# A hybrid decoder layer: program order for the load queue of the mixer, five weight pieces ahead, deferred stores, rotary tables first, norms and adaLN as small streams

## The chip, the cores and the metric

The kernel runs on one core of a Trainium2 chip. The metric is the device time of one execution in microseconds. TensorE (PE in the profile), VectorE (DVE), ScalarE (ACT), GpSimd (POOL) and SyncE (SP) run side by side; SP issues nearly all DMA transfers, in the order of its instruction queue.

## The reference

One layer, sequence S = 2048, width D = 1024, float32 throughout, cut to what matters:

```python
mod = silu(c) @ w_ada + b_ada                      # 6 vectors of 1024
shift1, scale1, gate1, shift2, scale2, gate2 = split(mod, 6)
h = rmsnorm(x, norm1_w) * (1 + scale1) + shift1
q, k, v, z, xbc, dt_raw = split(h @ w_in)          # 512, 128, 128, 512, 1024, 8 columns
q, k = rope(q, positions), rope(k, positions)
attn = sliding_window_attention(q, k, v, sinks)    # 8 heads, window 128
xbc = silu(causal_depthwise_conv(xbc, conv_w, conv_b))
xs, B, C = split(xbc)
dt = softplus(dt_raw + dt_bias)
y = ssd_chunked_scan(xs, dt, A, B, C, d_skip) * silu(z)
y = group_rmsnorm(y) * ssm_norm_w
x = x + gate1 * (concat(attn, y) @ w_out)
h = rmsnorm(x, norm2_w) * (1 + scale2) + shift2
x = x + gate2 * ((silu(h @ w_gate) * (h @ w_up)) @ w_down)   # inner width 2816
return rmsnorm(x, final_norm_w)
```

## The kernel before

The sequence is cut into four blocks of 512 tokens (`b` = 0 to 3). Activations lie with channels on the partitions: `h` is a list of eight slices of 128 channels, each a pair of tiles (a rounded part and the remainder), and every dense product is three matmuls, high by high, high by low, low by high (`mm3`, lines 237 to 240).

**Mixer phase.** For each block `norm1` makes `h`; then `queries`, `keys_values`, `convolved` and `gated` multiply it with the columns of `w_in`. Their results (q, k/v, convolved channels, z) go to DRAM. `attentions` and `ssds` read them back by tiles of 128 tokens as side streams; their results go to DRAM too (`spill`), and `out_proj` reads them for the output projection, which leaves `mid` (the residual stream) and a running sum of squares for the second norm. All dense products use four PSUM banks (`dense`); each side stream step uses one of four others (`side_bank`). `out_proj` of blocks 2 and 3 and the attention and scan that they need run beside the FFN.

**Weights** come in pieces (`weight`, line 222): at first use a piece is loaded raw, ACT makes the rounded part, POOL the remainder, and the pair is stored to DRAM; later blocks load the pair. There are six buffers for pairs (`SPLIT`) and five for raw pieces (`RAW`). The functions ask for a piece where they use it.

**Order.** Each of the functions is a Python generator. `run(main, ratio)` steps the dense stream; after each step `tick` counts down delayed actions (`pending`), steps the remaining adaLN columns once, and steps the side streams `ratio` times on average. Inside `manual_schedule` blocks the named engines keep the program's order: PE in the mixer, and PE, DVE and SP in the first norm. Everything else is ordered by a planner, which simulates the program with its own costs: SP in the mixer, all engines in the FFN, and DVE, ACT and POOL almost everywhere.

**First norm** (`first_norm`, line 929). x of block 0 is loaded; ACT squares it and PE sums the squares with 64 two-column matmuls (line 942); `root_of` and `spread` make the factor. The adaLN columns for shift1 and scale1 (`ada`, line 151: a load of 512 KB and one long DVE reduction, line 154) are made slice by slice between the modulations (lines 274 to 277). Then `rope_tables` (line 177) makes sine and cosine on DVE, which `rope` (lines 321 to 324) needs.

**The other 32 adaLN columns** (`ada_later`, line 156) are two loads of 256 KB and two reductions each (lines 160 and 165), through two buffers per half.

**FFN.** `operands` makes combinations of the normed blocks, `quads` the up projection (seven products in place of eight, lines 803 to 805), `down` the down projection; lines 709 and 772 load `spill` and `mid`.

Of the kernel before, what the change touches and what calls it, by code (L numbers as in the profile page):

```python
# [17 lines left out]
P = 128  # L18
# [12 lines left out]
TMP, M1, M2, M4 = 9, 3, 8, 4  # L31
# [11 lines left out]
def hymba_layer(ctx, tc, xT, crow, pos, wada, vecs, rows, wq, wkv, wz, wx, wo, wgu, wd4, wd2, outT):  # L43
# [29 lines left out]

    class tiles:
# [14 lines left out]
    common, extra = tiles(sb, M1, M2, M4), tiles(xp, 3, 10, 4)  # L89
# [7 lines left out]
    def const(shape, name, dt=F32, pool=sb):  # L97
        return pool.tile(shape, dt, name=name, tag=name, bufs=1)
# [57 lines left out]
    def ada_later(i):  # L156
# [4 lines left out]
        for _ in range(3):  # L161
            yield
# [14 lines left out]
    def rope_tables():  # L177
# [6 lines left out]
        for dst, turn in ((sin, 0.0), (cos, 0.25)):  # L184
# [8 lines left out]
            nc.scalar.activation(dst.rearrange("p t j -> p (t j)"), r, AF.Sin)  # L193

# [27 lines left out]
    def weight(src, n, key, store):  # L222
# [12 lines left out]
        return hi, lo  # L235

# [35 lines left out]
    def modulated(x, bc, scale, shift, into):  # L272
        h = tmp()
        nc.vector.scalar_tensor_tensor(h, x, scale, bc, ALU.mult, ALU.mult)
        hi, lo = into
        nc.scalar.activation(hi, h, AF.Identity, bias=shift)
        nc.vector.scalar_tensor_tensor(lo, h, shift, hi.bitcast(F32), ALU.add, ALU.subtract)  # L277
        return hi, lo
# [47 lines left out]
    def tokens(b, h, name, srcs, n, toks):  # L326
# [3 lines left out]
        for kp in range(KT // 2):  # L330
            whi, wlo = weight(srcs[kp], 2 * n, (name, kp), b == (0 if name[0] == "z" else 1) and toks[-1] == NT - 1)
# [10 lines left out]
    def queries(b, h):  # L342
        if b == 0:
            qb = [dense() for _ in range(NT)]
            for kp in range(KT // 2):
                ws = first_ws[kp] if kp < len(first_ws) else [weight(wq[c][kp], 512, (f"q{c}", kp), False)
                                                              for c in range(2)]
# [9 lines left out]
            for t, ps in enumerate(qb):  # L357
                q = extra.m2()
                rope(q, ps, 8, t)
                nc.sync.dma_start(q_d[t], q)  # L360
            return
        for part in range(2):
            for t, ps in (yield from tokens(b, h, f"q{part}", wq[part], 256, range(NT))):
                q = staged()
                rope(q, ps, 4, b * NT + t)
                nc.sync.dma_start(q_d[b * NT + t][:, part * 256:part * 256 + 256], q)
            yield

    def keys_values(b, h):
        dt_of[b] = small([P, NT, 8], "dt", 3)  # L370
        for half in range(2):
            for t, ps in (yield from tokens(b, h, "kv", wkv, 264, (2 * half, 2 * half + 1))):
# [4 lines left out]
                nc.sync.dma_start(kv_d[b * NT + t], kv)  # L377
            yield

    def convolved(b, h):  # L380
        for c in range(8):
            ps = dense()
            for half in range(2):
                if half:
                    yield
                whi, wlo = weight(wx[c, half], T, ("x", c, half), b == 0)
# [16 lines left out]
            nc.sync.dma_start(xs_d[b][c], o)  # L403
            yield

    def gated(b, h):
        for part in range(2):
            for t, ps in (yield from tokens(b, h, f"z{part}", wz[part], 256, range(NT))):
# [3 lines left out]
                nc.sync.dma_start(z_d[b * NT + t][:, part * 256:part * 256 + 256], z)  # L412
# [50 lines left out]
    def attentions(b, m):  # L463
        late = []

        def values_of(sms, slots, t):
# [8 lines left out]
            def sums(half):  # L475
# [3 lines left out]
                if half:  # L479
                    nc.sync.dma_start(spill[b][0:4, :, t * P:(t + 1) * P].rearrange("c p t -> p c t"),  # L480
                                      got["out"].rearrange("p (c t) -> p c t", c=4))
            return turn, sums

        held = None
        for t in range(NT):
            gt = b * NT + t
            q, kv = m.m2(), m.m1()
            nc.sync.dma_start(kv, kv_d[gt])
            nc.sync.dma_start(q, q_d[gt])
# [19 lines left out]
            for j in range(4):  # L509
# [3 lines left out]
                if j == 3:  # L513
                    probabilities(st, sms, slots)
                yield
# [74 lines left out]
    def ssds(b, stepping, m):  # L590
        dt, ahi, alo, ex = yield from stepping
        ub = upper.unsqueeze(1).broadcast_to([P, 4, P])
# [21 lines left out]
        def turned(y, o, ts):  # L614
# [6 lines left out]
            nc.sync.dma_start(dst[4:8, :, ts].rearrange("c p t -> p c t"), o3)  # L621

        for t in range(NT):
            ts = slice(t * P, (t + 1) * P)
            xl, z = m.m4().bitcast(F32).rearrange("p h t -> p (h t)").rearrange("p (c t) -> p c t", c=8), m.m2()
            nc.sync.dma_start(xl, xs_d[b][:, :, ts].rearrange("c p t -> p c t"))
            nc.sync.dma_start(z, z_d[b * NT + t])
# [40 lines left out]
            yield  # L668
            st = bank("st", 1)
# [22 lines left out]
            nc.vector.tensor_scalar(ss, ss, 1.0 / 256, EPS, ALU.mult, ALU.add)  # L692
            rs = small([P, 2], "rs", 2)
# [11 lines left out]
    def out_proj(b, y_of, into, bank_of, norm=None):  # L705
        mix = []
        for c in range(KT):
            m = tmp()
            nc.sync.dma_start(m, spill[b][c])
            mix.append(split(m, into(c)))  # L710
            if c % 4 == 3:
                yield
        acc = tmp()
        for c in range(KT):
            ps = bank_of(c)
            for half in range(2):
                if half:
                    yield
                whi, wlo = weight(wo[c, half], T, ("o", c, half), b == 0)
# [4 lines left out]
            x = tmp()  # L724
            nc.sync.dma_start(x, xT[b, c])
            nc.vector.scalar_tensor_tensor(x, ps, gate1[:, c:c + 1], x, ALU.mult, ALU.add)
            nc.sync.dma_start(mid[b][c], x)
            square_into(acc, x, c == 0)
            yield

        def root():
            y_of[b] = rstd(acc, st=norm and norm())
        if norm is None:
# [447 lines left out]
```

## Time and profile before

| | |
|---|---|
| median of 3 runs | 2439.05 us (2437.32 to 2443.29) |
| profiled execution, its own time | 2434.49 us |
| its span in the profile | 2432.8 us |
| mean granted PE clock | 0.965 |
| DMA traffic | 403.82 MB, mean 166 GB/s |

In the profile's groups "d<-w,hl" is a product of activations with a weight piece that gives tokens on the partitions (q, k/v, z), "d<-hl,w" one that gives channels (convolution). "issue to landing" of a transfer is from SP's instruction to its arrival. The idle time before an instruction is put down to what ended it.

### The profile page before, as it was taken

What the parts mean: (1) busy time and instruction counts of PE and PEld (TensorE: products, weight loads), DVE (VectorE), ACT (ScalarE), POOL (GpSimd) and SP (SyncE); (2) the same over time, 40 slices, a digit from 0 to 9 for tenths busy, and PEclk for the clock granted to TensorE, in tenths of its full rate; (3) what the DMA queues carried; (4) which work ended last, traced back from release to release, by engine and by line L of the source; (5) the groups of instructions that cost most, each with busy time, mean ns of one, the idle gap of its engine ahead of it and who ended that gap; (6) DMA issues with size and microseconds to landing.
All of it is one profiled execution on the core that took longest, in us unless ns stands there. A gap on an engine that the chain in (4) does not pass through costs nothing.

```text
span 2432.8 us, 33013 instructions
## 1 busy us (share of the span) xinstructions
PE 2261.8 (93%) x11254; PEld 1891.9 (78%) x11254; DVE 1461.9 (60%) x2519; ACT 967.3 (40%) x2004; POOL 1262.3 (52%) x1249
## 2 busy tenths in 40 slices
PE   6587999999999799999999999899899999999996
PEld 5567989887988588888887877677688888878785
DVE  7876874764445965578675434438855555554544
ACT  2354552655245545433334323224333333333332
POOL 3653743534122864679885234137766666643432
PEclk9798999999999799999999999999899999999998
DMA  7699866868874322233235555764322222263441
GB/s 274 210 331 316 294 228 204 279 218 275 287 241 159 96 78 83 81 111 100 88 95 167 197 177 158 249 206 136 130 87 84 86 79 78 78 228 98 145 157 53
DMA packets 244457, 403.82 MB, mean 166 GB/s; under 512 B 21952, under 2 KB 68032, under 8 KB 244288
## 3 DMA queue, kind: packets, MB, share of 16 engines
q1 hardware_dynamic: 243136, 400.66, 50.0%
q8 instruction: 89, 1.46, 0.2%
q10 hardware_dynamic: 1152, 1.05, 0.1%
q14 instruction: 80, 0.66, 0.1%
HBM read 307.19 MB, written 94.44 MB: 165 GB/s over the span
## 4 chain that ended last, share of the span: by engine, by line
PE 77%; DVE 8%; DMA 5%; issue 4%; POOL 3%; ACT 3%; SPq 1%; POOLq 0%; DVEq 0%; ACTq 0%
PE d L238 11%; PE d L240 11%; PE d L239 11%; PE d L803 8%; PE d L805 8%; PE d L804 8%; PE am L238 1%; PE am L239 1%; PE am L240 1%; POOL w L231 1%; PE at L574 1%; DMA t<-act 1%; DMA t<-in_xT_dram 1%; PE sm L683 1%; PE st L803 1%
## 5 line engine op out<-in xcount | busy, mean ns | idle before, releaser
L752 ACT ACTIVATE w<-raw 128x512 fp32r<-128x512 f32 x308 | 193.5, 630 | 531.7 <-PE d L240 251.0
L803 PE MATMUL d<-b,w 128*128 128x512 f32 x924 | 372.7, 405 | 17.4 <-ACT b L783 9.6
L804 PE MATMUL d<-b,w 128*128 128x512 f32 x924 | 370.8, 401 | 7.2 <-DVE b L779 5.1
L805 PE MATMUL d<-b,w 128*128 128x512 f32 x924 | 368.9, 399 | 0.0
L238 PE MATMUL d<-a,w 128*128 128x512 f32 (+1 forms) x720 | 281.1, 398 | 12.4 <-ACT a L871 11.5
L239 PE MATMUL d<-a,w 128*128 128x512 f32 (+1 forms) x720 | 281.5, 391 | 1.7 <-DVE a L747 1.7
L240 PE MATMUL d<-a,w 128*128 128x512 f32 (+1 forms) x720 | 282.3, 392 | 0.0
L753 POOL TENSOR_TENSOR w<-raw,w 128x512 fp32r<-128x512 f32 x88 | 120.1, 1365 | 304.8 <-ACT w L752 292.0
L753 POOL TENSOR_TENSOR w<-s,w 128x512 fp32r<-128x512 f32 x132 | 188.6, 1429 | 126.1 <-ACT w L752 117.6
L882 DVE SCALAR_TENSOR_TENSOR x<-d,mod,x 128x512 f32<-128x512 f32 (+1 forms) x182 | 130.9, 725 | 197.6 <-PE d L240 197.3
L238 PE MATMUL d<-w,hl 128*128 128x256 f32 (+1 forms) x640 | 194.8, 304 | 43.3 <-DVE s L322 19.9
L803 PEld LDWEIGHTS d<-b,w 128*128 128x128 f32 x924 | 175.9, 191 | 60.6 <-ACT b L783 13.3
L753 DVE TENSOR_TENSOR w<-raw,w 128x512 fp32r<-128x512 f32 x220 | 191.1, 869 | 43.3 <-ACT w L752 40.7
L804 PEld LDWEIGHTS d<-b,w 128*128 128x128 f32 x924 | 176.4, 191 | 46.7 <-DVE b L779 6.8
L805 PEld LDWEIGHTS d<-b,w 128*128 128x128 f32 x924 | 176.5, 191 | 39.9
L240 PE MATMUL d<-w,hl 128*128 128x256 f32 (+1 forms) x640 | 190.8, 298 | 4.6 <-DVE hl L277 4.6
L239 PE MATMUL d<-w,hl 128*128 128x256 f32 (+1 forms) x640 | 189.7, 296 | 0.0
L238 PEld LDWEIGHTS d<-a,w 128*128 128x128 f32 x720 | 137.1, 191 | 47.5 <-ACT a L871 15.5
L238 PEld LDWEIGHTS d<-w,hl 128*128 128x128 f32 x640 | 130.8, 204 | 48.4 <-issue 20.9
L239 PEld LDWEIGHTS d<-a,w 128*128 128x128 f32 x720 | 136.8, 190 | 34.4 <-DVE a L747 2.8
L248 POOL TENSOR_TENSOR t<-t 128x512 f32<-128x512 f32 (+1 forms) x84 | 106.7, 1271 | 108.5 <-ACT t L247 104.8
L240 PEld LDWEIGHTS d<-a,w 128*128 128x128 f32 x720 | 136.2, 189 | 30.3
(311 smaller groups left out, 5427.7 us busy)
## 6 DMA issues: line engine op xcount, KB each, us to landing
raw<-in_wgu_dram SPq DMA_DIRECT2D x176, 256.0 KB, 2.7
raw<-in_wd_dram SPq DMA_DIRECT2D x176, 256.0 KB, 2.7
w<-w_x SPq DMA_DIRECT2D x48, 512.0 KB, 4.9
w<-w_o SPq DMA_DIRECT2D x48, 512.0 KB, 4.6
act<-t SPq DMA_DIRECT2D x88, 256.0 KB, 2.1
t<-act SPq DMA_DIRECT2D x88, 256.0 KB, 4.7
t<-in_xT_dram SPq DMA_DIRECT2D x80, 256.0 KB, 4.3
aw<-in_wada_dram SPq DMA_DIRECT2D x64, 256.0 KB, 3.8
```

The costliest lines, as they stand in the source:

```text
L231: nc.gpsimd.tensor_tensor(lo, raw[:, :n], hi.bitcast(F32), ALU.subtract)
L238: nc.tensor.matmul(out, ahi, bhi, start=first, stop=False)
L239: nc.tensor.matmul(out, ahi, blo, start=False, stop=False)
L240: mm3.last = nc.tensor.matmul(out, alo, bhi, start=False, stop=last)
L248: eng.tensor_tensor(acc, acc, sq, ALU.add)
L574: nc.tensor.transpose(ps[:, (2 * s + r) * P:(2 * s + r + 1) * P], sm[:, r, s, :], ident)
L752: nc.scalar.activation(hi, x, AF.Copy)
L753: eng.tensor_tensor(lo, x, hi.bitcast(F32), ALU.subtract)
L803: nc.tensor.matmul(out, ahi, bhi, start=first and k == 0, stop=False, skip_group_check=True)
L804: nc.tensor.matmul(out, ahi, blo, start=False, stop=False, skip_group_check=True)
L805: mm3.last = nc.tensor.matmul(out, alo, bhi, start=False, stop=k == 3, skip_group_check=True)
L882: nc.vector.scalar_tensor_tensor(x, ps, gate2[:, c:c + 1], x, ALU.mult, ALU.add)
```

## The change

- The first norm makes the sine table before anything else on DVE and the cosine table between the sum of squares and the root. The squares are summed by seven DVE adds and four matmuls. q of block 0 goes to two side banks and two dense banks.
- In the mixer phase SP, too, keeps the program's order. All weight pieces of the phase are listed in `plan`, in the order of use; `take_w` hands out the next one and issues loads until five are ahead.
- Stores in the mixer (`put`) are issued one to three steps after the instruction that makes their data.
- `norm1` becomes a stream: one x load per step, then three steps, the root, four steps, and the eight modulations in two halves, each behind a permission (`free`) and behind its four loads. The factor is copied to SBUF. adaLN columns wait four steps in place of three between loads and reductions; they start after q of block 0, behind the last modulation on DVE.
- Side streams load one tile ahead; `out_proj` gets its inputs from a stream of loads (`loads`) and loads x ahead of its matmuls; the dt steps run inside `ssds`.
- Sums of squares have a tile of their own; there are eight temporaries in place of nine, and nine `m2` tiles of the mixer's extra pool in place of ten.

The diff, cut to its core:

```diff
-TMP, M1, M2, M4 = 9, 3, 8, 4
+TMP, M1, M2, M4 = 8, 3, 8, 4
...
+    def sums():
+        return big("acc", 1, pool=fw)
...
-    common, extra = tiles(sb, M1, M2, M4), tiles(xp, 3, 10, 4)
+    common, extra = tiles(sb, M1, M2, M4), tiles(xp, 3, 9, 4)
...
-        for _ in range(3):
+        for _ in range(4):
             yield
...
-            nc.sync.dma_start(split_d[key], two[:, :, :n].bitcast(F32))
+            put(split_d[key], two[:, :, :n].bitcast(F32), 3)
...
+    pending, mixer_phase = [], [True]
+
+    def put(dst, src, ticks):
+        if mixer_phase[0]:
+            pending.append([ticks, lambda: nc.sync.dma_start(dst, src)])
+        else:
+            nc.sync.dma_start(dst, src)
...
+    planned, ahead = plan(), []
+
+    def fetch(n):
+        for _ in range(n):
+            spec = next(planned, None)
+            if spec is not None:
+                ahead.append(weight(*spec))
+
+    def take_w(n=1):
+        fetch(n - len(ahead))
+        got = [ahead.pop(0) for _ in range(n)]
+        fetch(SPLIT - n - len(ahead))
+        return got
...
-    def norm1(b, h):
-        acc = tmp()
+    def norm1(b, h, free):
+        acc, xs = sums(), []
         for d in range(KT):
-            square_into(acc, load_x(b, d), d == 0)
-        yield
+            xs.append(load_x(b, d))
+            yield
+            if d:
+                square_into(acc, xs[d - 1], d == 1)
+        square_into(acc, xs[-1], False)
+        for _ in range(3):
+            yield
         y = rstd(acc)
-        yield
-        bc = spread(y)
-        for d in range(KT):
-            h.append(modulated(load_x(b, d), bc, scl1[:, d:d + 1], sh1[:, d:d + 1], operand()))
-        yield
+        for _ in range(4):
+            yield
+        bc, ps = const([P, T], "bc", pool=ip, bufs=1), spread(y)
+        nc.scalar.copy(bc, ps)
+        for half in range(2):
+            while free[0] <= half:
+                yield
+            xs = [load_x(b, 4 * half + i) for i in range(4)]
+            yield
+            for i in range(4):
+                d = 4 * half + i
+                h.append(modulated(xs[i], bc, scl1[:, d:d + 1], sh1[:, d:d + 1], operand()))
+                if i % 2:
+                    yield
...
-            qb = [dense() for _ in range(NT)]
+            qb = [side_bank(2), side_bank(3), dense(), dense()]
...
-        held = None
+        def load(t):
+            q, kv = m.m2(), m.m1()
+            nc.sync.dma_start(kv, kv_d[b * NT + t])
+            nc.sync.dma_start(q, q_d[b * NT + t])
+            return q, kv
+
+        held, nxt = None, load(0)
+        yield
+        yield
...
+                if j == 2 and t + 1 < NT:
+                    nxt = load(t + 1)
...
     def first_norm():
-        st, h, x0, ws = side_bank(0), [], [], []
+        accs, h, x0, tables = [tmp(), tmp()], [], [], rope_tables()
+        next(tables)
+        for i in range(2):
+            silu_c(i)
...
-        for d in range(2):
-            ada(8 + d, common.m4)
-            ada(d, extra.m4)
         for d in range(KT):
-            sq = tmp()
-            nc.scalar.activation(sq, x0[d], AF.Square)
-            for t in range(NT):
-                nc.tensor.matmul(st[:, 2 * t:2 * t + 2], sq[:, t * P:(t + 1) * P], ones[:, 0:2],
-                                 start=d == 0 and t == 0, stop=d == KT - 1 and t == NT - 1, skip_group_check=True)
+            square_into(accs[d % 2], x0[d], d < 2, nc.vector)
+        acc = accs[0]
+        nc.vector.tensor_tensor(acc, acc, accs[1], ALU.add)
+        st = side_bank(0)
+        for t in range(NT):
+            nc.tensor.matmul(st[:, 2 * t:2 * t + 2], acc[:, t * P:(t + 1) * P], ones[:, 0:2], start=True, stop=True)
+        next(tables)
+        ada(8, common.m4)
+        ada(0, extra.m4)
+        fetch(2)
         y = root_of(st, NT)
...
-        if ada_rest:
-            next(ada_rest[0], None)
+        for g in list(background):
+            if next(g, g) is g:
+                background.remove(g)
...
-    with tc.manual_schedule(engines={mybir.EngineType.PE}):
-        run(queries(0, h), 0)
-        with tc.issue_after(last_load.ins):
-            nxt = norm_ahead(1, (17, 21))
-        rest = rest_of_ada()
-        ada_rest.append(rest)
-        run(keys_values(0, h), 0)
-        prepared(0)
+    with tc.manual_schedule(engines={mybir.EngineType.PE, mybir.EngineType.SP}):
+        with tc.issue_after(first_done.ins):
+            run(queries(0, h), 0)
+            nxt, free = norm_ahead(1, 1)
+            background.append(rest_of_ada())
+            run(keys_values(0, h), 0)
...
+        while background or pending:
+            tick(0)
+        finish(att)
+        while pending:
+            tick(0)
+    mixer_phase[0] = False
```

More of the change, by code (lines that the diff above doesn't have):

```diff
@@ L371, in keys_values @@
         for half in range(2):
-            for t, ps in (yield from tokens(b, h, "kv", wkv, 264, (2 * half, 2 * half + 1))):
+            for t, ps in (yield from tokens(h, 264, (2 * half, 2 * half + 1))):
                 kv = staged()
@@ L385, in convolved @@
                     yield
[L386 removed]
+                (whi, wlo), = take_w()
                 for i in range(4):
@@ L407, in gated @@
         for part in range(2):
-            for t, ps in (yield from tokens(b, h, f"z{part}", wz[part], 256, range(NT))):
+            for t, ps in (yield from tokens(h, 256, range(NT))):
                 z, th = staged(), big("s", 3, pool=fw)[:, 0:256]
@@ L718, in out_proj @@
                     yield
-                whi, wlo = weight(wo[c, half], T, ("o", c, half), b == 0)
+                whi, wlo = weights(c, half)
                 for i in range(4):
```

235 lines of the change are left out of this document (136 added, 99 removed).

## The prediction

> **What bounds the kernel now.** I read the profile's page first, then the busy times of the engines by stage, then who waits for whom inside the stages.
>
> ```profile
> span 2432.8 us, 33013 instructions
> PE 2261.8 (93%) x11254; PEld 1891.9 (78%) x11254; DVE 1461.9 (60%) x2519; ACT 967.3 (40%) x2004; POOL 1262.3 (52%) x1249
> PE   6587999999999799999999999899899999999996
> PEclk9798999999999799999999999999899999999998
> ```
>
> TensorE (PE) is busy for 2261.8 of 2432.8 us, so 171 us of idle time is all that reordering can win directly, and the slices put most of it in the first four (61 us each). The next view cuts the span at the stages: norm of block 0; its q projection; a hole; k/v, convolution and z gate of block 0; q and k/v of block 1; two long stretches of blocks 1 to 3; the change-over to the FFN; three stretches of FFN. Columns: stretch, length, busy us (instructions) of PE, PEld, DVE, ACT and POOL, granted PE clock, DMA share, GB/s.
>
> ```profile
> 0.00:31.00 31.00, 15.86 (x66) 14.23 (x66) 17.11 (x37) 8.60 (x14) 7.54 (x51) 1.00 0.89 340
> 31.00:79.00 48.00, 35.27 (x192) 32.17 (x192) 42.25 (x71) 13.07 (x22) 17.31 (x11) 0.82 0.61 196
> 79.00:98.00 19.00, 0.00 (x0) 0.00 (x0) 18.30 (x30) 6.31 (x10) 10.36 (x8) 0.60 0.61 201
> 98.00:216.00 118.00, 95.42 (x555) 84.77 (x556) 83.34 (x208) 57.88 (x132) 73.67 (x76) 0.91 0.92 316
> 216.00:281.00 65.00, 55.87 (x397) 53.84 (x396) 50.21 (x133) 26.68 (x62) 42.48 (x45) 0.87 0.83 275
> 281.00:603.00 322.00, 307.69 (x1925) 273.81 (x1925) 202.92 (x476) 171.59 (x435) 143.09 (x248) 0.98 0.75 249
> 603.00:782.00 179.00, 177.51 (x1118) 158.39 (x1119) 83.55 (x247) 72.76 (x175) 32.64 (x57) 1.00 0.70 231
> 782.00:832.00 50.00, 32.91 (x129) 22.73 (x128) 47.80 (x59) 33.04 (x74) 38.76 (x26) 0.73 0.32 99
> 832.00:1297.00 465.00, 464.76 (x2283) 387.46 (x2282) 306.71 (x447) 206.65 (x466) 340.37 (x329) 1.00 0.29 92
> 1297.00:1740.00 443.00, 413.42 (x1721) 327.81 (x1719) 241.02 (x334) 144.24 (x238) 191.29 (x136) 0.96 0.54 176
> 1740.00:2433.00 693.00, 663.06 (x2880) 536.64 (x2880) 368.67 (x483) 226.44 (x382) 364.80 (x268) 0.98 0.34 112
> ```
>
> Idle PE by stage: 15.1, 12.7, 19.0, 22.6, 9.1, 14.3, 1.5, 17.1, 0.2, 29.6 and 29.9 us. Block 0 up to the first work of block 1 (216 us) holds 69 of the 171, and it is where DMA is nearest its end (316 GB/s, share 0.92). Who ended PE's waits from 98.5 to 282 us (total, times, longest):
>
> ```profile
> PE d L238 <- DVE s L322: 19.9, 2, 19.6
> PE d L238 <- DVE so L411: 8.6, 2, 6.7
> PE am L493 <- DMA m<-kv: 8.4, 1, 8.4
> PE at L574 <- DVE m L578: 5.4, 1, 5.4
> PE d L238 <- ACT hl L276: 3.6, 2, 2.4
> PE d L240 <- DVE hl L277: 2.6, 3, 1.6
> ```
>
> and three of those from 281 to 782 us, the largest and the only two that a DMA ended:
>
> ```profile
> PE st L617 <- ACT m L697: 4.8, 1, 4.8
> PE at L501 <- DMA m<-q: 0.9, 1, 0.9
> PE d L238 <- DMA w<-w_o: 0.3, 1, 0.3
> ```
>
> Block 0 waits for tables, loads and late evictions; blocks 1 to 3 hardly wait for a transfer (1.2 us in 501). A better order of loads can win early and has next to nothing to win later, where it can only lose.
>
> **The change, part by part.** *Rotary tables first.* The 19.6 us hole ends at the rope of q (L322): k/v cannot start because all four dense banks hold q, and DVE makes the tables only then, with adaLN reductions between. Quiet steps of the tables cost
>
> ```profile
> L191 DVE SCALAR_TENSOR_TENSOR s<-s 128x512 f32<-128x512 f32 x2 | 1.4, 684 | 0.0
> L187 DVE TENSOR_SCALAR s<-s 128x512 f32<-128x512 f32 x1 | 0.4, 427 | 0.0
> ```
>
> so sine or cosine is 4 x 0.43 + 3 x 0.68 = 3.8 us. Sine goes where DVE waits for x; cosine goes between the sum of squares and the root, on the path (3.8 us, counted next). Moreover q of block 0 now takes two side banks, so two dense banks are free and k/v starts at once: -19.6 us. If the cover failed, the rope alone (16 DVE operations on half of L187's elements, so at most 16 x 0.43 = 7 us) would delay the second half of k/v, which needs the two banks behind it.
>
> *First norm.*
>
> ```profile
> 8.33 4.98 ACT L940 ACTIVATE t<-m 128x512 f32<-128x512 f32 x8
> 9.09 13.79 PE L942 MATMUL am<-ones,t 128*128 128x2 f32 x64 [9.09 <-ACT t L940]
> ```
>
> Sixty-four small matmuls end at 22.9 us; in their place are seven adds of DVE (0.68 each, 4.8 us, beside the squares that end at 13.3) and four matmuls, about 16 us. Then cosine (3.8) and two adaLN reductions come before the root: about 22 us, 1 earlier. The loop over the eight slices of h follows, bound by DVE:
>
> ```profile
> L154 DVE CUSTOM_DVE_ANT_0 m<-m,csil,vec 128x1024 f32<-128x1024 f32 x12 | 20.1, 1707 | 0.0
> L277 DVE SCALAR_TENSOR_TENSOR hl<-t,mod,hl 128x512 fp32r<-128x512 f32 x8 | 7.6, 955 | 4.1 <-ACT hl L276 3.7
> L274 DVE SCALAR_TENSOR_TENSOR t<-m,scl,at 128x512 f32<-128x512 f32 x8 | 5.9, 744 | 0.1
> ```
>
> These three are 33.6 of DVE's 42.25 us there; the rest is mostly the later adaLN columns, which now queue behind the last slice. Two L154 more move in behind the root (+3.4), and the wait for ACT that those columns partly filled opens again (3.7 us in the row, up to twice that). Net -1 us, between -5 and +3; with the root -2.
>
> *adaLN and the first x loads as streams.* One 256 KB load pair per five steps of the mixer, where before
>
> ```profile
> L160 SPq DMA_DIRECT2D aw<-in_wada_dram x22: 327/328/382, 16.5 to 96.9; - x22
> L160 SPq DMA_DIRECT2D aw<-in_wada_dram x27: 327/656/2020, 102.6 to 213.6; - x27
> L165 DVE CUSTOM_DVE_ANT_0 aw<-aw,csil,vec 128x512 f32<-128x512 f32 x14 | 15.2, 1085 | 4.9 <-DMA aw<-in_wada_dram 4.9
> L165 DVE CUSTOM_DVE_ANT_0 aw<-aw,csil,part 128x512 f32<-128x512 f32 x13 | 11.4, 876 | 6.9 <-DMA aw<-in_wada_dram 6.9
> ```
>
> (first two: issues up to 98 us and from 98 to 216; then DVE in 98 to 216). Of 49 loads ahead of block 1 about 11 stay: block 0 has 28 steps after q. From 98 to 216 DVE loses some 16 us of work and the 11.8 us that it stood in order before a reduction; DVE's late evictions (8.6, 5.4) hang on that. Bytes: 0.316 x 118 = 37.3 MB moved in that stretch; less 27 x 0.262, plus 11 x 0.262, plus about 3.5 MB (k/v and convolution weights, x) that went during the q stage and the hole: 36.6 MB. How fast can they go? The fastest 20 us:
>
> ```profile
> 140.00:160.00 20.00, 18.61 (x86) 15.01 (x85) 13.01 (x32) 14.87 (x37) 13.66 (x16) 1.00 1.04 381
> ```
>
> At 381 GB/s it is 96 us, at the stretch's own 316 it is 116; PE's own busy time is 95.4. I take 105, the middle, for both limits would have to be met exactly for 96: -13 us. The Trainium skill, "DMA: Bandwidth & Descriptors", section Specifications, puts HBM at about 358 GB/s for a core; by that 36.6 MB take an estimated 102 us and the gain here could not pass 16. The trace's 381 over 20 us is above it, so the measurement sets the floor.
>
> *Norm of block 1* is ready by steps, four slices before the z gate ends: the 3.6 + 2.6 us of waits on hl go, -5. The norm's factor is now copied out of its bank, one ACT operation per block (4.98 / 8 = 0.6 us, with ACT busy 57.88 of 118). Late next is the side attention's DVE work (L574 behind L578), whose loads now come two steps early; POOL keeps all its work (73.67 of 118).
>
> *Queue in program order, five pieces ahead, stores deferred.* SP now holds every load of the mixer behind whatever store or load waits ahead of it: weights, x, q/k/v of the side streams. What covers it:
>
> ```profile
> 166.15 0.40 PE L238 MATMUL d<-hl,w 128*128 128x512 f32 x1
> 166.39 0.39 PE L239 MATMUL d<-hl,w 128*128 128x512 f32 x1
> w<-w_x SPq DMA_DIRECT2D x45, 512.0 KB, 4.8
> SPq L226 <- PE d L240: 99.7, 55, 4.2
> ```
>
> A piece is 12 matmuls at a pitch of 0.23, 2.8 us, so five are 13.8 us; a load lands 4.8 us after issue, which leaves 9 us for holds. SP's most common wait (for PE to free a weight buffer; its rows are those of 281 to 782 us) was 1.8 us on average, 4.2 at most. So the queue is covered, and its cost lies between 0 and, if the 38 displaced adaLN loads (10 MB, 26 us at 381 GB/s) found no room, 26 us; DMA's free quarter of 501 us makes me take 5. The k/v pieces are half as long, hence not 0.
>
> *Rest.* One temporary buffer less, running sums and the norm's broadcast in tiles of their own, the dt steps of blocks 2 and 3 moved into the FFN (some 20 tiny DVE operations beside 465 us in which PE idles 0.2): 0, within -8 to +8. The change-over at 782 is untouched: 0, from -17 (its whole idle time) to +5.
>
> **The sum** is -19.6 - 2 - 13 - 5 + 5 = -35 us. The profiled execution took 2434.49 us, 4.6 below the median of the runs shown, 2439.05 (2437.32 to 2443.29): 2399.5 against the one, 2404 against the other, which I predict.
>
> **Rivals.** *Fuller gain.* If adaLN was what kept block 0 from PE's pace, 118 becomes 95 (-23), the waits on hl go whole (-6), and, DVE being ahead, the change-over closes as well (-17): with -22 from the start, -68, 2371. For it: DVE at 47.80 of 50 us there. Against it: DMA at 0.92 before, and that change-over's work is untouched. Chance 0.14.
>
> *Bytes decide.* The stretch stays at 316 GB/s and 116 us (-2), the displaced loads cost 14 of their 26: -22 - 2 + 14 = -10, 2429. For it the 0.92; against it that much of the waiting was for DVE. Chance 0.10, half of it too small to tell.
>
> *The queue becomes the bound, slower.* From 281 to 782 us there are 128 steps of 3.9 us. Once SP's holds and issues take longer than a step, the lead of five is used up and PE waits at each piece; before, other loads passed the one that waited. If each step then loses 0.6 us, 77 us go against the 40 won: +37, 2476. Decisive is a hold over 9 us, or a mean of over 3.9 per step; the rows show 1.8 for the common one. A rule of the skill is its ground: "DMA: Bandwidth & Descriptors", section on the anatomy of one DMA, says that the DMA engines do not wait on semaphores, so every wait stands in the issuing sequencer. Chance 0.16.
>
> **Numbers.** The forecast itself has 0.60 (2380 to 2419). About 0.3%, 7 us, is what a measurement can tell. Faster: 0.60 + 0.14 + 0.05 = 0.79; the same 0.05; slower 0.16. The range 2360 to 2450 leaves out the end of the fuller gain and most of the slower rival.
>
> **What would show it.** Right: no PE hole before k/v, k/v near 77 us and block 1 near 182; some 11 adaLN loads by then; from there stage lengths within 3% of those above. Wrong: PE waits in blocks 1 to 3 that end at a weight load, SP holds of over 9 us, or a k/v stage that waits for its banks.

## The result and the profile after

The changed kernel takes 2465.65 us (median of 4 runs, 2460.41 to 2470.41) against 2438.19 us of the kernel before beside it (2432.82 to 2443.29): a ratio of 1.0112, 95% interval 1.0082 to 1.0143. It is slower by 27.5 us where 35 us less were forecast. The profiled execution spans 2465.6 us, 32.8 more than the one before.

The top of its profile page, with the same lines as were shown of before:

```profile
span 2465.6 us, 32901 instructions
PE 2263.2 (92%) x11198; PEld 1886.1 (76%) x11198; DVE 1430.0 (58%) x2526; ACT 970.5 (39%) x2009; POOL 1271.5 (52%) x1249
PE   3788999897899699999999999998899999999896
PEclk9899999998999799999999999998899999999998
```

PE has the same work (2263.2 us against 2261.8), so what was lost is idle time: 202 us in place of 171. The slices (61.6 us each) say where: the first is emptier than before, the second and fourth are fuller, the eighth, tenth and eleventh show 8, 7 and 8 where 9s stood, and the fourteenth, the change-over, a 6 for a 7. Busy time by stage (same columns as before), cut at the first and last dense matmuls of this kernel's stages:

```profile
0.00:39.00 39.00, 3.91 (x10) 2.28 (x10) 28.30 (x52) 15.09 (x22) 11.57 (x53) 1.00 0.64 238
83.50:104.00 20.50, 13.46 (x98) 12.95 (x98) 6.87 (x27) 6.11 (x11) 13.33 (x18) 0.83 0.59 205
257.80:580.00 322.20, 301.69 (x1862) 267.55 (x1861) 208.25 (x488) 159.77 (x397) 142.11 (x230) 0.97 0.77 257
580.00:621.00 41.00, 23.62 (x132) 19.23 (x131) 20.14 (x46) 20.63 (x57) 9.81 (x17) 0.73 0.49 170
621.00:666.70 45.70, 39.73 (x300) 38.51 (x300) 19.23 (x79) 6.56 (x14) 11.05 (x25) 0.94 0.81 273
```

and the k/v stage of block 3 in the kernel before:

```profile
633.00:646.00 13.00, 13.00 (x108) 12.85 (x107) 10.00 (x40) 3.88 (x9) 5.07 (x12) 1.00 1.02 385
```

The row to look at is 580 to 621. It holds 132 matmuls in 41 us, nearly all of them the side streams' own, and PE is idle for 17 us of it at a granted clock of 0.73. Before, this stretch, from the output projection of block 0 to q of block 3, lasted 5.5 us. In the next row k/v of block 3 takes 19.8 us of the 45.7, from its first matmul to its last; before it took 13.1 with PE busy throughout. The row from 83.5 is k/v of block 0, 20.5 us of which PE idles 7.

Set against before stage by stage (by the starts of dense products in the two traces; a stage ends where its last three matmuls start), the 32.8 us and the forecast's terms are:

| stretch | forecast | measured |
|---|---|---|
| start to k/v of block 0 (98.3, now 83.6) | -21.6 | -14.7 |
| k/v of block 0 to q of block 1 (117.9 us, now 114.3) | -13 | -3.6 |
| q of block 1 to the end of the output projection of block 0 (381.5, now 382.1) | 0 (-5 and +5) | +0.6 |
| that end to q of block 3 (5.5, now 41.0) | 0 | +35.5 |
| q of block 3 to the end of its z gate (178.1, now 179.7) | 0 | +1.6 |
| change-over and FFN (1651.5, now 1664.9) | 0 | +13.4 |
| sum | -34.6 | +32.8 |

Up to the fourth row the change is 17.7 us ahead. Three causes stand in the trace. The first is the start. ACT's rows, then DVE's, then POOL's (start, duration, what it was idle for):

```profile
12.01 1.28 ACT L197 ACT_TABLE_LOAD   x1
14.99 1.28 ACT L148 ACT_TABLE_LOAD   x1
18.49 1.28 ACT L197 ACT_TABLE_LOAD   x1
```

```profile
16.94 0.69 DVE L149 SCALAR_TENSOR_TENSOR csil<-s,csil 128x512 f32<-128x512 f32 x1 [4.23 <-ACT s L148]
17.55 5.87 DVE L310 TENSOR_TENSOR t<-t 128x512 f32<-128x512 f32 x6
```

```profile
18.03 3.03 POOL L239 TENSOR_TENSOR w<-raw,w 128x512 fp32r<-128x512 f32 x2 [12.34 <-ACT w L238]
```

The sine (L197) now stands between the two halves of silu(c) (L148), so ACT changes its function table, changes back, and changes again. DVE, in program order, waits 4.23 us for the second half with six of the adds of squares behind it, and these take 5.87 us in place of the 3.75 that they take in a run below, because POOL's two subtractions start among them (last section). The sum of squares ends at 24.1 us, and q starts at 39.2 where it was 32.4.

The second is SP. What its queue waited for, first in the first 300 us, then from 300 to 860 (total, times, longest):

```profile
SPq L250 <- POOL m L400: 24.6, 3, 18.8
```

```profile
SPq L250 <- DVE sx L477: 100.9, 18, 12.1
SPq L250 <- DVE so L486: 37.0, 15, 5.3
SPq L250 <- DVE t L822: 35.1, 12, 6.2
SPq L250 <- POOL so L400: 31.0, 20, 7.2
```

Line 250 is the deferred store. The store of q of block 0 waits 18.8 us for the rope, and the raw weights of the convolution stand behind it:

```profile
83.94 8.34 SPq L250 DMA_DIRECT2D q<-m  x4
94.31 0.35 SPq L237 DMA_DIRECT2D raw<-in_wx_dram  x1
```

At k/v of block 3 it is the same with short pieces, SP's issues and then PE's waits from 578 to 668 us:

```profile
645.39 0.50 SPq L234 DMA_DIRECT2D w<-w_kv  x1
649.54 3.72 SPq L250 DMA_DIRECT2D q<-so  x4
653.31 0.42 SPq L807 DMA_DIRECT2D t<-mix  x1
653.83 1.25 SPq L234 DMA_DIRECT2D w<-w_kv  x2
```

```profile
PE at L656 <- DVE m L660: 5.7, 2, 4.3
PE d L300 <- DMA w<-w_kv: 5.6, 3, 3.5
PE st L715 <- ACT m L797: 4.8, 1, 4.8
```

From 645.9 to 653.8 no weight is issued, because stores of q wait for the rope; a lead of five pieces is 13.8 us elsewhere and half of that here. The other two of these waits belong to the third cause: attention and scan steps (L656, L715) that run bare from 580 to 621, each waiting for its own last step.

Those steps are left over from before. The program runs `finish(mix1)`, which steps the side streams of block 1 to their end. A block's attention and scan are 62 side steps now and were 57, for `attentions` and `ssds` begin with two and three empty steps that give their first loads a lead. At the ratio of 1.1 side steps per dense step, more of block 1 is left when the dense work beside it ends. In the change, `finish(mix1)` also moved ahead of q of block 3, which now runs at ratio 0; before, q of block 3 ran beside the side streams. The change-over begins in the same way, with what is left of the attention of block 2: the FFN's first product starts 9.3 us after the last matmul of the z gate ends, where it was 5.4, which is 4 of the 13.4 us in the table.

### The profile page after: what moved, and what is told of

It is laid out like the page before. It is cut to its first block, busy times and chain, and to the rows that moved or that the text cites. A ratio compares the mean times of both kernels' runs of the same rounds, so it can differ in the third digit from the quotient of the medians.

```text
span 2465.6 us, 32901 instructions
## 1 busy us (share of the span) xinstructions
PE 2263.2 (92%) x11198; PEld 1886.1 (76%) x11198; DVE 1430.0 (58%) x2526; ACT 970.5 (39%) x2009; POOL 1271.5 (52%) x1249
## 4 chain that ended last, share of the span: by engine, by line
PE 65%; DVE 7%; DMA 5%; ACT 2%; POOL 2%; issue 2%; SPq 1%; DVEq 0%; POOLq 0%; ACTq 0%
PE d L902 8%; PE d L904 8%; PE d L903 8%; PE d L300 7%; PE d L301 7%; PE d L302 7%; DMA t<-in_xT_dram 1%; PE am L300 1%; PE am L301 1%; PE am L302 1%; DVE b L878 1%; PE sm L902 1%; PE st L902 1%; PE st L904 1%; PE sm L904 1%
## 5 line engine op out<-in xcount | busy, mean ns | idle before, releaser
L300 PE MATMUL d<-a,w 128*128 128x512 f32 (+1 forms) x720 | 282.6, 402 | 24.9 <-ACT a L970 15.3
L300 PE MATMUL d<-w,hl 128*128 128x256 f32 (+1 forms) x608 | 178.9, 294 | 11.9 <-ACT w L238 6.2
L301 PE MATMUL d<-w,hl 128*128 128x256 f32 (+1 forms) x608 | 176.6, 290 | 12.2 <-POOL w L239 12.2
L300 PEld LDWEIGHTS d<-a,w 128*128 128x128 f32 x720 | 138.7, 193 | 60.8 <-ACT a L970 18.8
L302 PE MATMUL d<-w,hl 128*128 128x256 f32 (+1 forms) x608 | 174.9, 288 | 0.8 <-DVE hl L339 0.8
L310 POOL TENSOR_TENSOR acc<-acc,t 128x512 f32<-128x512 f32 (+1 forms) x84 | 106.0, 1262 | 124.1 <-ACT t L309 117.3
L301 PEld LDWEIGHTS d<-a,w 128*128 128x128 f32 x720 | 138.3, 192 | 34.5 <-DVE a L846 2.9
L239 POOL TENSOR_TENSOR w<-raw,w 128x512 fp32r<-128x512 f32 (+1 forms) x72 | 98.9, 1381 | 124.8 <-ACT w L238 92.8
L851 ACT ACTIVATE w<-s 128x512 fp32r<-128x512 f32 x176 | 110.2, 628 | 130.8 <-PE d L904 94.6
```

The source lines that it names most:

```text
L239: nc.gpsimd.tensor_tensor(lo, raw[:, :n], hi.bitcast(F32), ALU.subtract)
L300: nc.tensor.matmul(out, ahi, bhi, start=first, stop=False)
L301: nc.tensor.matmul(out, ahi, blo, start=False, stop=False)
L302: mm3.last = nc.tensor.matmul(out, alo, bhi, start=False, stop=last)
L310: eng.tensor_tensor(acc, acc, sq, ALU.add)
L851: nc.scalar.activation(hi, x, AF.Copy)
```

## The experiments

Ratios are against the kernel before on the same chip. Its medians there lie between 2434.6 and 2438.2 us, so a difference of less than some 4 us between the medians of two runs below tells nothing.

**The planner orders the queue again.** All else is as in the changed kernel.

```diff
-    with tc.manual_schedule(engines={mybir.EngineType.PE, mybir.EngineType.SP}):
+    with tc.manual_schedule(engines={mybir.EngineType.PE}):
```

> The changed kernel with SP given back to the planner in the mixer; weights five ahead, deferred stores, streams and tables stay. Queue: the changed kernel loses its time to holds of SP, so this comes back to 2440 or below, with k/v of block 0 some 6 us shorter and the hole at 580 us smaller. Bare steps: that hole (35 us of swing against the kernel before) stays, only the hold at the q stores of block 0 goes; time 2455 to 2465.

Measured: 2437.58 us, 1.0006 (0.9994 to 1.0018). The queue in program order costs 28 us. By stage: k/v of block 0 to q of block 1 takes 105.8 us (114.3 in the changed kernel), q and k/v of block 1 54.2 (59.9), from there to the end of the output projection of block 0 316.9 (322.2), q and k/v of block 3 36.8 (45.7). The stretch between, from the output projection to q of block 3, hardly moves; this kernel's rows:

```profile
562.50:602.80 40.30, 24.94 (x133) 21.08 (x132) 17.28 (x40) 20.41 (x57) 6.36 (x17) 0.72 0.25 80
602.80:639.60 36.80, 36.80 (x300) 36.70 (x300) 15.93 (x69) 6.02 (x12) 8.86 (x22) 0.98 0.88 293
```

40.3 us of bare side steps with DMA at 0.25: the stretch does not come from the queue. The time is what the first theory gave, the stretch what the second did. The planner reorders more than the stores: it issues 39 adaLN loads ahead of q of block 1, where program order issues 11.

**Stores three steps late, in program order.** If the holds are the cost, later stores find their data made.

```diff
-                put(q_d[t], q, 1)
+                put(q_d[t], q, 3)
...
-            put(xs_d[b][c], o, 2)
+            put(xs_d[b][c], o, 3)
```

(and q of the other blocks, k/v, z and `mid` from 1 to 3)

> The changed kernel, SP in program order, with the stores of q, k/v, z, convolved channels and mid issued three steps after their data's instructions in place of one (two for the convolved channels). Holds: SP stands before stores whose rope or eviction is still in POOL's or DVE's queue, and the weight loads behind come late; with later stores 10 to 20 of the 28 us that the planner's order won come back, time 2450 (2443 to 2457), and k/v of block 3 goes from 19 to under 15 us. If the loss is not in the stores but in loads that wait for buffers: time 2460 to 2470.

Measured: 2447.93 us, 1.0048 (1.0028 to 1.0067), 17.7 less than the changed kernel. K/v of block 0 takes 11.7 us to the first convolution (20.6 in the changed kernel), k/v of block 3 12.5 from its first matmul to its last (19.8). So some two thirds of the queue's cost were stores that waited for their data one or two steps after it was asked for; the ten runs spread from 2440.6 to 2456.9 us, so the share is rough. The stretch of bare steps is again 40 us.

**A lead of two pieces.** The same mechanism from the other side.

```diff
-        fetch(SPLIT - n - len(ahead))
+        fetch(SPLIT - 3 - n - len(ahead))
```

> The changed kernel with weights two pieces ahead in place of five; all else as there. By the prediction's account of cover: two pieces of 2.8 us are 5.5 us of work against 5 us from issue to landing, so any hold of SP reaches PE: 2510 (2490 to 2560). Rival (the pieces' lead matters little, since holds by stores delay five as well as two): 2460 to 2485.

Measured: 2584.80 us, 1.0615 (1.0599 to 1.0631), beyond the forecast. PE's waits from 100 to 800 us:

```profile
PE d L300 <- ACT w L238: 35.9, 12, 6.8
PE d L300 <- DMA w<-w_x: 21.2, 8, 7.0
PE d L300 <- DMA w<-w_kv: 16.4, 4, 6.5
```

With a lead below the holds PE waits for weights in every stage behind k/v of block 0, for raw pieces and their split (L238) most. This is what the slower rival of the prediction described, and five pieces keep it to a few places.

**More side steps per dense step.** If the stretch of 41 us is side steps left over, a higher ratio spends them beside dense work.

```diff
-MIX, RATIO_UP = 1.1, 0.6
+MIX, RATIO_UP = 1.35, 0.6
```

> The changed kernel with 1.35 side steps per dense step in blocks 1 and 2 in place of 1.1 (MIX); order and queue stay. Late side streams: the change adds five yields to each block's attention and scan (62 steps for 57) and takes the eight steps of block 3's q from them, so some 14 steps of block 1 are left over and run alone; at 1.35 none are left, q of block 3 follows the output projection of block 0 within 10 us, and the time falls by 25 to 35, to 2435 (2428 to 2445). Rival (a side step costs PE the same 2 to 3 us wherever it stands, as the run with q of block 3 put ahead suggested): the hole goes and blocks 1 and 2 grow by as much, time 2455 to 2470.

Measured: 2456.36 us, 1.0077 (1.0053 to 1.0102). The stretch is gone (the output projection of block 0 ends at 606.9 us, q of block 3 starts at 607.6), but that end came 27 us later, and the time is the one that the rival gave: with the queue in program order the stages before grew by most of what the stretch had taken.

> 1.35 side steps and SP's order in the mixer given back to the planner. Queue and late side streams are separate and add up: 28 from the queue and 30 from the side streams, 2407 (2398 to 2416). If they are one and the same loss: 2433 to 2440.

The same edit with the planner's queue: 2416.91 us, 0.9916 (0.9887 to 0.9944), 20.7 less than with the queue alone.

```profile
515.00:580.00 65.00, 60.43 (x310) 50.37 (x309) 19.70 (x42) 27.05 (x69) 25.10 (x32) 0.99 0.77 248
580.00:620.00 40.00, 37.36 (x291) 36.62 (x290) 21.25 (x71) 8.98 (x15) 10.22 (x21) 0.96 0.91 311
```

The row from 580 to 620 now has q and k/v of block 3, 291 matmuls in place of 132. The output projection ends 17.5 us later than with ratio 1.1, and 40 us of bare steps are gone.

> SP's order given to the planner, both Sin together, as in the run of all three, with 1.2 side steps in place of 1.35. If the leftover of block 1 sets the cost: a few steps run bare again, 2420 (2414 to 2428). If denser side steps cost what they save: 2405 to 2413.

Ratio 1.2 with planner and one function table (below): 2434.95 us, 1.0003 (0.9993 to 1.0013), with 23.5 us of bare steps left (581.9 to 605.4). At 1.35 there are none, so the length of the stretch is a matter of how many steps are left. The time is not: it is beyond both expectations and no better than at 1.1. From q of block 1 to q of block 3 it takes 419 us here, 411 with the planner's queue at 1.1, and 388 to 391 at 1.35 with all empty steps. At 1.2 the dense stages grew by more than the stretch lost; why they did not at 1.35 is open.

**q of block 3 beside the side streams, as before.** `finish(mix1)` goes behind q, and the loads for the second output projection go in fewer steps.

```diff
+        run(queries(3, h), MIX)
         finish(mix1)
...
-        run(queries(3, h), 0)
```

> The changed kernel with the q products of block 3 put back ahead of the forced end of block 1's side streams, as in the kernel before; the eight inputs of block 1's output projection are then loaded during k/v of block 3. Bare steps (in the changed kernel the side streams of block 1 run alone from 580 to 621 us, where the kernel before had q of block 3 beside them): the 41 us between the end of block 0's output projection and q of block 3 fall to under 12, and the time comes to 2436, between 2428 and 2445. Queue (SP's program order makes PE wait everywhere): the steps are as long as before wherever they stand, time 2460 to 2470.

Measured: 2474.66 us, 1.0163 (1.0140 to 1.0185), slower, against the forecast. q took 45 us (24.9 in the changed kernel), 20 us of bare steps stayed behind it, and the second output projection took 61 us in place of 51. PE's waits from 560 to 670 us:

```profile
PE d L315 <- POOL acc L310: 9.5, 1, 9.5
PE d L300 <- ACT m L224: 5.7, 1, 5.7
```

The first is the norm of block 3, whose sum is not made in time, the second the split of the output projection's inputs. In the changed kernel both were done under the bare steps. So the place of `finish(mix1)` alone does not explain the loss. This run does not show what it would be worth with those two done in time.

**Without the five empty steps.** They are taken out of the changed kernel, of the one with the planner's queue, and of the best one.

```diff
         held, nxt = None, load(0)
-        yield
-        yield
...
         next_xs, next_z = load_xs(0), load_z(0)
-        yield
-        yield
         dt, ahi, alo, ex = yield from stepping
-        yield
```

> The changed kernel without the five empty steps per block that attention and scan take after their first loads (two and three); MIX stays 1.1. Late side streams: ten steps fewer stand in front of the forced end of block 1's streams, so the hole between the output projection of block 0 and q of block 3 falls from 41 us to about 15, and the time to 2445 (2435 to 2455). Rival (the hole is the missing cover of block 3's q, not the number of steps): the hole stays above 30, time 2458 to 2470.

Program order: 2478.29 us, 1.0179 (1.0164 to 1.0194), slower than the changed kernel and than both expectations. The bare stretch falls from 41 to 22 us, and the part behind the last z gate from 1664.9 to 1655.6, but PE waits once in block 0 and once at 672 us for k/v of a side stream, first from 98 to 215, then from 632 to 690 us:

```profile
PE am L571 <- DMA m<-kv: 11.9, 1, 11.9
```

```profile
PE am L571 <- DMA m<-kv: 11.1, 1, 11.1
```

> The run with the planner's queue, without the five empty steps per block that lead the attention and the scan. Theory A, the empty steps only lengthen the side streams: with the planner placing the loads, the bare stretch behind the output projection of block 0 shrinks from 40 to about 21 us, the part from the end of the last z gate goes from 1664 back towards 1655, and 2437.6 becomes about 2412 (2403 to 2422). Rival B, the empty steps are what lets the loads of the side streams arrive in time, whoever places them: PE waits of 5 to 11 us that end at loads of q, k/v or z stand in place of the bare steps, and the time is 2435 to 2450.

Planner's queue: 2437.13 us, 1.0007 (0.9997 to 1.0017), no gain over 2437.58, as rival B said. The bare stretch is 23.4 us (40.3), the last part 1658 (1665.2), but q of block 1 starts at 213.7 us where it was 191.4.

> The run with planner, step ratio 1.35 and one function table, without the five empty steps. Theory A: nothing is left over at ratio 1.35 already, so only the last part, from the end of the last z gate, gains: 2413.3 becomes about 2402 (2395 to 2410). Rival B, loads come late without the empty steps: 2412 to 2425.

Planner, ratio 1.35, one table: 2441.12 us, 1.0025 (1.0015 to 1.0036), 28 more than with the empty steps and beyond both expectations. PE's waits from 98 to 215 us:

```profile
PE am L575 <- DMA m<-kv: 11.5, 1, 11.5
PE am L304 <- DVE k_ring L579: 5.3, 1, 5.3
PE at L658 <- DVE m L587: 4.0, 1, 4.0
```

The first attention of block 0 reads k and v that were stored just before. Without the empty steps PE, in order, stands for 11.5 us at their transpose (2.1 with them). q of block 1 starts at 210.3 us where it was 188.9. The theory that the steps only cost is wrong for block 0.

**Empty steps in block 0 alone.**

```diff
         held, nxt = None, load(0)
-        yield
-        yield
+        if b == 0:
+            yield
+            yield
```

(and the three of `ssds` in the same way)

> The run with planner, step ratio 1.35 and one function table, with the empty steps kept in block 0 alone. Theory A, only block 0's first side steps need them (there a PE wait of 11.5 us at a k/v load and what followed cost 21 us by q of block 1 when they were gone): block 0 as in the run with all empty steps, and the last part, from the end of the last z gate, shorter by the 9 us that both runs without them show: 2413.3 becomes 2404 (2398 to 2410). Rival B, each block needs them, as the waits of the scan for its first tile suggest: 2412 to 2425.

With planner, ratio 1.35 and one table: 2402.64 us, 0.9877 (0.9853 to 0.9902), the fastest kernel of this study. It is 10.6 us less by the medians than with all empty steps (the ratios, 0.9877 and 0.9894, differ by 4 us and their intervals overlap, so the size is rough). In the traces nearly all of it lies behind the last z gate: 2408.7 - 753.8 = 1654.9 us against 2418.8 - 754.7 = 1664.1. PE's wait between 1220 and 1330 us, where the FFN's first part changes to the next, first with all empty steps, then with those of block 0:

```profile
PE d L304 <- ACT a L974: 6.1, 1, 6.1
```

```profile
PE d L304 <- ACT a L977: 1.3, 1, 1.3
```

With all empty steps the scan's last load of z is issued at 1254.2 us, without those of the later blocks at 1213.5: that load comes 41 us earlier. That the side streams beside the FFN end sooner, and so leave less over, is a reading of this and was not tested by itself. Another 2.4 us lie at the change-over: the FFN's first product starts 5.4 us after the last z gate in place of 7.8.

> The run with the planner's queue and ratio 1.1, with the empty steps kept in block 0 alone. Theory A: no loss in block 0, the bare stretch behind the output projection of block 0 is 25 to 30 us in place of 40, the last part about 8 us shorter: 2437.6 becomes 2418 (2412 to 2426). Rival B: 2433 to 2445, the lost cover taking back what the stretch gives.

With the planner's queue at ratio 1.1: 2430.79 us, 0.9989 (0.9976 to 1.0002), 6.8 less than with all of them and between the two expectations. The last part is 1656.1 us, as forecast, but the bare stretch shrinks by 5 only, to 35.3. So 9 of the 13 us in the last part are the empty steps of the later blocks. The bare stretch owes them 5; the other 12 that it lost when all were gone came with those of block 0, where the steps have their use.

**One function table.** Sine's argument is kept, and both sines run together behind silu(c).

```diff
-        one(sin, 0.0)
+        r = one(0.0)
         yield
-        one(cos, 0.25)
+        act(sin, r)
+        act(cos, one(0.25))
```

> The changed kernel with the Sin of the sine table asked for only beside that of the cosine table, so that ACT does not change its function table between the two Tanh of silu(c). Late root (three table loads of 1.28 us on ACT and DVE's order delay the second half of silu(c) to 16.9 us and the sum of squares behind it to 24.1): the first matmul comes 5 us sooner, at 19, k/v of block 0 at 78 in place of 83.6, and the time is 2460, between 2456 and 2463. If adaLN loads or DVE's loop set the start instead: k/v stays at 83, time 2463 to 2468.

Measured: 2456.93 us, 1.0098 (1.0061 to 1.0135), 8.7 less than the changed kernel by the medians; by the ratios it is 3, and their intervals overlap, so the size is uncertain. The start is sooner beyond doubt: q at 34.2 us (39.2), k/v at 76.3 (83.6), q of block 1 at 188.6 (197.9). Its DVE rows:

```profile
11.95 0.69 DVE L149 SCALAR_TENSOR_TENSOR csil<-s,csil 128x512 f32<-128x512 f32 x1 [1.00 <-ACT s L148]
12.56 3.75 DVE L314 TENSOR_TENSOR t<-t 128x512 f32<-128x512 f32 x6
```

The wait of 4.23 is 1.00, and the six adds take 3.75 us in place of 5.87, for POOL starts after them.

**Tables first in the kernel before.** Only the early tables, in this form, and q of block 0 on two side banks.

```diff
-            qb = [dense() for _ in range(NT)]
+            qb = [side_bank(2), side_bank(3), dense(), dense()]
```

> The kernel before with one part of the change alone: both tables early (sine before silu(c), cosine before the root, both Sin together) and q of block 0 on two side banks. By the prediction's first step: the 19.6 us hole before k/v goes, less up to 4 us for a cosine on the path: k/v of block 0 at 83, block 1 16 us sooner, time 2422, between 2418 and 2428. Rival (the bytes of block 0 decide and take the gain back): k/v at 83 but block 1 less than 6 us sooner, time 2433 to 2440.

Measured: 2425.20 us, 0.9958 (0.9942 to 0.9974), 11 less than before. K/v of block 0 starts at 80.8 us, 17.5 earlier, and q of block 1 at 199.9, 16.3 earlier; the end of the last z gate is 13.7 earlier.

**All together.**

> SP's order given to the planner, 1.35 side steps, and both Sin together (no change of ACT's table inside silu(c)). If the three add up: 9 us below the run without the last, 2398 (2390 to 2408), faster than both kernels.

Planner, ratio 1.35, one table: 2413.26 us, 0.9894 (0.9864 to 0.9925). Here the one table brings 3.7 us over the run without it (2416.91), where 9 were expected; that is too little to tell from none.

> SP in program order with stores three steps late, 1.35 side steps, both Sin together. If later stores mend what was wrong with program order: 18 + 9 + 9 us below the changed kernel, or more since the hole closes further without holds, 2425 (2412 to 2435), within 12 of the same kernel with the planner's order (2413). If program order costs by itself: 2435 to 2450.

Program order with stores three steps late, ratio 1.35, one table: 2422.14 us, 0.9946 (0.9930 to 0.9963). A queue in program order can be faster than the kernel before; with the stores moved it is 9 behind the planner's.

## Why the prediction was wrong

**Rotary tables first (-19.6).** Right in mechanism. The hole is gone, and without the rest of the change k/v comes 17.5 us earlier; 11 us of the time are left of it at the end.

**First norm (-2, "about 22 us, 1 earlier").** Mis-sized: q came 6.8 us later. The step took the adds to lie beside the squares, and left out that the sine is an ACT function of its own: three table loads of 1.28 us and 4.23 us of DVE's wait in order. With both sines together, q is still 1.7 late; 2 us are lost at the first steps of the cosine, which take 1.49 and 1.41 us beside POOL in place of 0.43 each.

**The stretch from 118 to 105 us (-13).** The size can be reached, but not for the reason given. The prediction took the middle of 96 and 116 us, DMA at its fastest and at the stretch's own pace, and hung the gain on adaLN loads that go later. Of those 11 are issued by 198 us, as forecast (45 before), and yet the stretch takes 114.3. The rows of this stretch with the planner's queue, then in program order with later stores:

```profile
85.60:191.40 105.80, 93.11 (x545) 81.40 (x544) 89.06 (x189) 60.67 (x127) 80.33 (x79) 0.95 0.96 337
82.10:187.80 105.70, 92.15 (x545) 81.16 (x544) 60.11 (x137) 58.36 (x122) 73.60 (x80) 0.95 0.80 281
```

The first kernel still issues 39 adaLN loads ahead of q of block 1 (49 before) and the second 10, and both take 106 us. So most of the loads that were to go later cost nothing there, and the second kernel, at 281 GB/s, is not held by bytes; that 105 came out is in part luck. The 8.5 us above it are what program order costs in this stretch. What brought 118 down to 106 stays open. The early tables did not: with them alone it is 119.1.

**Norm of block 1 (-5).** q and k/v of block 1 went from 66.3 to 59.9 us, 6.4 less, and 54.2 without the queue's part; PE's waits for the slices of h there fall from 6.2 us to 0.8. Right.

**"So the queue is covered" (+5, between 0 and 26).** This step failed; the queue costs 28 us. It took the holds from one row, the wait for a free weight buffer, 1.8 us on average and 4.2 at most, in a trace where the planner had placed the stores. The same view of before (281 to 782 us) has rows of stores that wait for their data, the second with longer holds:

```profile
SPq L403 <- DVE sx L402: 37.3, 17, 4.4
SPq L234 <- POOL w L231: 23.9, 9, 7.9
```

In program order the first of these stores waits 100.9 us in 18, up to 12.1, the store of q of block 0 waits 18.8, and the weights wait behind them. Its caution that k/v pieces are half as long was the right place, with 9 us at q and k/v of block 3 alone. The slower rival had the sign and the mechanism, but not the form: it is no 0.6 us at each of 128 steps but a few places, 28 us where it asked for 77. That its 2476 lies near the measured 2465.65 is luck, since more of the loss came from the side steps. By the Trainium skill, "DMA: Bandwidth & Descriptors", section on the anatomy of one DMA, waits stand in the issuing sequencer; the rows of line 250 agree, with 100.9 us in 18 waits for one kind of store.

**"Rest: 0", and the change-over "untouched".** This is the larger failure, 35.5 + 13.4 = 49 us. The prediction listed the moved dt steps. It named the two steps by which the attention's loads come early, but put no cost on them, missed the three of `ssds`, and did not count that the steps beside dense work are dealt out by a ratio. Five more steps per block at the same ratio come out as a tail at each `finish`. Taken out, they cost more in block 0 than they bring; taken out of blocks 1 to 3, they bring 7 to 11 us by the medians, mostly behind the last z gate; and what they and the moved q leave over at block 1 is spent by a ratio of 1.35, which brings 20.7, while 1.2 brings nothing that can be told. How the 35.5 us divide between the steps and the place of `finish(mix1)` stays open, since putting q back also moved the norm and the loads that the bare steps had covered, and so do some 4 of the 13.4.

**The watch list** named PE waits at weight loads and SP holds of over 9 us; both came. It had no line for bare side steps, which cost most.

## What to carry to other kernels

Putting a queue in program order turns each store into a gate for the loads behind it: move stores past the latest maker of their data before counting how far ahead the loads are. Where side work is dealt out by a ratio, count its steps, for an empty one takes a turn as a full one does, and set the ratio again after each change, by trial of more than one value; keep a lead only where a load is really late. Before moving an activation function, look which function stands on either side of it.

## What the runs showed of the hardware

An ACT_TABLE_LOAD takes 1.28 us, and the ACTIVATE behind it starts within 0.01 us of its end (12.01 + 1.28, then 13.30), so a switch costs 1.28 here. The Trainium skill, "ScalarE: Activation LUTs", section "What ACT_TABLE_LOAD costs", gives the same load and about 1.38 us of drain beside it, 2.66 in all; the trace shows no drain.

DVE's adds of two SBUF tiles take 0.68 us each while POOL is quiet (they overlap: six in 3.75). In the changed kernel two of the six take more than twice that, beside POOL's two subtractions:

```profile
18.15 1.75 DVE L310 TENSOR_TENSOR t<-t 128x512 f32<-128x512 f32 x1
19.83 1.78 DVE L310 TENSOR_TENSOR t<-t 128x512 f32<-128x512 f32 x1
```

POOL's run from 18.03 to 19.35 and from 19.32 to 21.06; each of the two adds starts during one of them and ends 0.55 us after it. The Trainium skill, "SBUF — State Buffer", section "SBUF: two separate sides", has DVE, in an operation with two SBUF inputs, and GpSimd hold a shared pair of ports by turns, each for a whole instruction; the trace agrees.
